# A sparse expert stage between two transformer blocks: the first expert as a unit of its own, gate2 moved to the expert blocks, the late products behind the last down projection

## The chip, the cores and the metric

The kernel runs on 1 core of one Trainium2 chip. The metric is the time of one execution on the device in microseconds, the median of several. The core has a matrix engine (PE, its weight loads shown as PEld), a vector engine (DVE), a scalar engine (ACT), GpSimd (POOL) and a sync engine (SP); 16 DMA engines move data, by queues that SP and POOL fill in this kernel.

## What is computed

512 tokens of width 1024 go through a first block (a mixer, then 32 experts, 4 for each token) and a second block (attention, a gated recurrence, an MLP). The change lies in the experts:

```python
logits = xf @ w_router + b_router
top_val, top_idx = lax.top_k(logits, 4)          # of 32 experts
gates = jax.nn.softmax(top_val, axis=-1)
...
def expert_block(args):                          # 128 rows of one expert e
    xb, e = args
    hu = xb @ w_up[e] + b_up[e]                  # 1024 -> 2048
    x_glu = jnp.minimum(hu[:, :D_FF], 7.0)
    x_lin = jnp.clip(hu[:, D_FF:], -7.0, 7.0)
    act = x_glu * jax.nn.sigmoid(1.702 * x_glu) * (x_lin + 1.0)
    return act @ w_down[e] + b_down[e]           # 1024 -> 1024
ys = lax.map(expert_block, (xs, block_e)).reshape(n_pad, D)
out = segment_sum(ys * row_gate[:, None], row_tok, num_segments=T)
```

The first block then adds `gate2 * out` to the residual, where gate2 is a row of 1024 numbers that the condition gives.

## The kernel before, in words

**Stages.** The mixer runs to about 437 us, the expert stage from there to about 1528, the second block behind it. Everything in the expert stage is in float32. An expert's weights are 8 tiles of `w_up` and 4 of `w_down`, each 128 x 2048 (1 MB); all 32 experts have 384 tiles. `raw` (L296 to L302) fetches one on SP's queue into a ring of 13 buffers, so that a fetch waits until PE has used an older tile.

**Units and steps.** The experts are taken by rank (by how many tokens they have). `UNITS` (L36) lists units of one or two steps: a step is one expert with 128 rows (`_single`), two experts that share a block of 128 rows (`_pair`), or two blocks. Experts 0 and 1 are known by number; from rank 2 on SP reads the expert's number from `Ei` (L1277). For each step `expert_up` makes the up products (L1134, tile `bank_hu`) and the activation; then comes the down projection of the step *before* (`expert_down`, L1134, tile `bank_y`), so that the transposes of one step's activation (`transposed`, L1203, L1204, tile `aT`) are used one step later. At a unit's last step `hot_unit`, `block_rows` and `slots` make the one-hot columns of the next unit, and `gather_unit` gathers its tokens by 64 matmuls with the one-hot columns (L1145, 256 wide: two blocks). `expert_out` multiplies the result by the token's gate (ACT, L1223) into `yb`, and POOL scatters it into `y_d` (L1226), which has four slots for each token. After unit 1 stands a dynamic loop for experts with more rows (L1511; it runs no round here); ahead of it up to 10 tiles of the next unit are fetched.

**The end of the stage.** `expert_bias` loads the residual `xs` (4 tiles of 128 tokens, `h2h` in the rows) and adds the bias part. `add_slots` then loads 8 pairs of pieces of `y_d` by POOL's queue (L1456, tiles `h2l` and `xT`, three pairs of buffers in turn), adds the two (L1457), multiplies by gate2 (`g2bc`, L1458) and adds to `xs` (L1459), two pairs for each `xs`. The last two blocks do not go through `y_d`: `late_rows` transposes their one-hot columns (L1235), and `late_add` makes `yb` = y x gate x gate2 (L1246), splits it in a high and a low part (L1247 on ACT, L1248 on DVE), spreads both over the tokens by products into a `bank_hu` (L1251, L1252) and adds each bank to `xs` (L1253). It is called for the last but one block ahead of the last down projection, and for the last block behind it. Each bank is given back only by its add. The order on PE is that of the code (`pin`); DVE, ACT and POOL run their own queues in the order that the scheduler gives.

Of the kernel before, what the change touches and what calls it, by code (L numbers as in the profile page):

```python
# [7 lines left out]
F = mybir.dt.float32  # L8
# [23 lines left out]
def _pair(a, b, n):  # L32
# [3 lines left out]
UNITS = [  # L36
    [_single(0), _single(1)],
    [_pair(7, 25, 96), _pair(8, 26, 96)],
    [_pair(15, 16, 64), _single(4)],
    [_pair(9, 27, 96), _pair(17, 18, 64)],  # L40
    [[[(2, 0, 128, 0)], [(2, 0, 64, 128), (14, 64, 64, 0)]]],
    [_pair(10, 28, 96), _pair(19, 20, 64)],
    [_pair(11, 29, 96), _single(5)],
    [_pair(12, 30, 96), _pair(21, 22, 64)],
    [[[(3, 0, 128, 0)], [(6, 0, 96, 0), (3, 96, 32, 128)]]],
# [211 lines left out]
def tile_block(ctx, tc, A, out, dbg=None):  # L257
# [846 lines left out]
    hot_unit()  # L1104
    hot0 = [hot_cols(Z[:, :, 64 + b], hot_of(b, (b, 0, 128, 0))) for b in range(2)]
    sel0 = mt([128, 2], "sel0", 1, FR)
# [44 lines left out]

    def gather_unit():
        return gather_T([hots[-1][:, tb] for tb in range(NTB)], 256)

# [43 lines left out]
    def transposed(src):  # L1198
        t = mt([128, 8, 128], "aT", 3, F, mo)
        for k0 in (0, 4):  # L1200
            pt = trbank()
            for k in range(4):
                pin(pe.transpose(pt[:, k * 128:(k + 1) * 128], src[:, (k0 + k) * 128:(k0 + k + 1) * 128], ident))  # L1203
            (vec.tensor_copy if k0 else act.copy)(out=t[:, k0:k0 + 4, :], in_=pt.rearrange("p (k t) -> p k t", k=4))  # L1204
        return t
# [13 lines left out]
    def expert_out(y, sl):  # L1219

        yb = mt([128, 1024], "yb", 2, F, mo)
        for n in range(2):
            act.activation(out=yb[:, n * 512:n * 512 + 512], in_=y[n], func=AF.Copy, scale=sl[1])  # L1223

# [5 lines left out]
    def late_rows(b):  # L1230

        hotT = mt([128, 1024], "ma", 3, FR, mo)[:, 0:512]
        pt = trbank()
        for tb in range(NTB):
            pin(pe.matmul(out=pt[:, tbs[tb]], lhsT=hots[-1][:, tb, 128 * b:128 * b + 128].bitcast(F), rhs=ident,  # L1235
                          start=True, stop=True))
        act.copy(out=hotT, in_=pt)
        return hotT

    def late_add(y, gc, hotT):  # L1240

        yh, yl = (mt([128, 8, 128], "aT", 3, FR, mo).rearrange("p a b -> p (a b)") for _ in range(2))
        t_ = mt([128, 1024], "yb", 2, F, mo)
        for h in range(2):
            hs = slice(h * 512, h * 512 + 512)
            vec.scalar_tensor_tensor(out=t_[:, hs], in0=y[h], scalar=gc, in1=g2bc[:, hs], op0=OP.mult, op1=OP.mult)  # L1246
            act.copy(out=yh[:, hs], in_=t_[:, hs])  # L1247
            vec.tensor_tensor(out=yl[:, hs], in0=t_[:, hs], in1=yh.bitcast(F)[:, hs], op=OP.subtract)  # L1248
            for tb in range(NTB):
                o = pbank("hu")  # L1250
                pin(pe.matmul(out=o, lhsT=hotT[:, tbs[tb]], rhs=yh[:, hs], start=True, stop=False))  # L1251
                pin(pe.matmul(out=o, lhsT=hotT[:, tbs[tb]], rhs=yl[:, hs], start=False, stop=True))  # L1252
                vec.tensor_tensor(out=xs[tb][:, hs], in0=o, in1=xs[tb][:, hs], op=OP.add)  # L1253

# [60 lines left out]
    for src, k in [(ranked(0)[0], k) for k in range(8)] + [(ranked(0)[1], k) for k in range(4)]:  # L1315
        ready[src, k] = raw(src(k))
    X = gather_unit()

# [35 lines left out]
    for n, col in enumerate((RC("p32"), kcol[:, 1:2])):  # L1354
# [14 lines left out]
                             op0=OP.mult, op1=OP.add)  # L1369
    sls = [slots([(0, hot0[b], lambda tb: R[:, tb, b, :])]) for b in range(2)]  # L1370

# [74 lines left out]

    def add_slots():

        spare = mt([128, 8, 256], "xT", 2).rearrange("p a b -> p (a b)")
        pairs_ = [[h2_("l", 0), h2_("l", 1)], [h2_("l", 2), h2_("l", 3)], [spare[:, 0:1024], spare[:, 1024:2048]]]  # L1450
        for tb in range(NTB):
            for j in (0, 2):
                y = pairs_[0]
                pairs_.append(pairs_.pop(0))
                for i, t in enumerate(y):
                    pool.dma_start(out=t, in_=y_d[(j + i) * T + tb * 128:(j + i) * T + tb * 128 + 128, :])  # L1456
                vec.tensor_tensor(out=y[0], in0=y[0], in1=y[1], op=OP.add)  # L1457
                vec.tensor_tensor(out=y[0], in0=y[0], in1=g2bc, op=OP.mult)  # L1458
                vec.tensor_tensor(out=xs[tb], in0=xs[tb], in1=y[0], op=OP.add)  # L1459

    LOOP = 1
    prev = None
    for u, unit in enumerate(UNITS):
        nxt = [blk for step in UNITS[u + 1] for blk in step] if u + 1 < len(UNITS) else []
        sls_, b0 = [], 0
        for n, step in enumerate(unit):
# [9 lines left out]
            if n + 1 == len(unit) and nxt:  # L1476
                X = gather_unit()
            finish = lambda: None
            late = not nxt and n
            if late:  # L1480
                hotT = late_rows(n - 1)
            if prev is not None:
                for y, sl in zip(expert_down(*prev[:2]), prev[2]):
                    finish()
                    if late:
                        late_add(y, sl[1], hotT)
                    else:
                        finish = expert_out(y, sl)
            if u != LOOP or n + 1 < len(unit):
                finish()  # L1490
            prev = (down, [((transposed(a),) + rows[1:], of) for a, (rows, of) in zip(au, blocks)], sls[b0:b0 + len(step)])
            b0 += len(step)
            if not nxt and n == 0:
                expert_bias()
                add_slots()
        sls = sls_
        if u == LOOP:
# [539 lines left out]
```

## Time and profile before

| | |
|---|---|
| median of 3 runs | 2861.84 us (2855.33 to 2865.29) |
| the profiled execution | 2863.78 us, its span 2861.8 |
| busy: PE, DVE, ACT, POOL | 92%, 50%, 27%, 17% |
| chain that ended last: PE, DMA, DVE | 46%, 15%, 12% |
| L1134 products of up / of down | 573.5 / 259.7 us |

A row of the timeline is the start, the time from the first to the last instruction of a run of alike ones, and in brackets how long the engine had idled and what ended that. A row of windows gives the busy time of each engine in a stretch, the clock granted to PE, the share in which the DMA engines were busy, and GB/s.

### The profile page before, as it was taken

The numbers are of one execution on the slowest core, as the hardware profiler recorded it, in microseconds if no ns is written. First come the engines' busy times: TensorE is split into PE (matmuls) and PEld (weight loads), VectorE is DVE, ScalarE is ACT, GpSimd is POOL, SyncE is SP. The second block draws the span as 40 slices with busy tenths as digits, with TensorE's granted clock in tenths as the row PEclk, the third lists the DMA queues.
The fourth block names the chain that finished last, engine by engine and source line by source line (L and its number), as shares of the span: only waits on it lengthen the run. The fifth ranks groups of instructions, "written<-read, shape, count | busy, mean of one in ns | idle before, by whom it ended". The sixth has DMA issues, their size and how long they took to land.

```text
span 2861.8 us, 37210 instructions
## 1 busy us (share of the span) xinstructions
PE 2620.6 (92%) x14592; PEld 1705.2 (60%) x14592; DVE 1419.4 (50%) x2470; ACT 766.5 (27%) x1312; POOL 483.3 (17%) x371
## 2 busy tenths in 40 slices
PE   7999998988999999999948898999988898799997
PEld 4777774433445334334315567777867677688886
DVE  4865573211112111111254668676478888855456
ACT  4432430000000100001004444232235555333231
POOL 1000000000000000000013213333251334422223
PEclk9999998999999999999978998999999899799999
DMA  7355457799999999999983424564323222232231
GB/s 269 111 178 185 149 184 291 306 421 389 421 421 372 422 421 421 421 421 370 421 346 130 157 81 151 175 225 150 98 77 105 72 86 86 70 107 95 89 103 52
DMA packets 128241, 647.34 MB, mean 226 GB/s; under 512 B 16272, under 2 KB 17252, under 8 KB 78912
## 3 DMA queue, kind: packets, MB, share of 16 engines
q1 hardware_dynamic: 121936, 628.07, 57.9%
q0 software_dynamic: 5984, 16.35, 1.5%
q8 instruction: 116, 1.90, 0.3%
q14 instruction: 61, 0.50, 0.1%
q10 hardware_dynamic: 144, 0.52, 0.0%
HBM read 624.42 MB, written 22.12 MB: 226 GB/s over the span
## 4 chain that ended last, share of the span: by engine, by line
PE 46%; DMA 15%; DVE 12%; ACT 2%; issue 2%; POOL 0%; DVEq 0%; SPq 0%; ACTq 0%
PE bank_hu L1134 11%; DMA raw<-in_w_up_dram 6%; PE bank_y L1134 5%; PE bank_d L319 5%; PE bank_d L321 4%; PE bank_d L320 4%; DMA raw<-in_w_down_dram 4%; PE bank_u L321 3%; PE bank_u L319 3%; PE bank_u L320 3%; DVE wl L315 2%; DMA graw<-in_ada_w_dram 2%; PE bank_tr L1145 2%; DMA raw<-in_ada_w_dram 1%; DVE vv L1951 1%
## 5 line engine op out<-in xcount | busy, mean ns | idle before, releaser
L1134 PE MATMUL bank_hu<-raw,xT 128*32 128x512 f32 (+2 forms) x3456 | 573.5, 598 | 13.7 <-DMA raw<-in_w_up_dram 13.7
L1134 PEld LDWEIGHTS bank_hu<-raw,xT 128*32 128x32 f32 (+2 forms) x3456 | 203.2, 124 | 363.1 <-issue 323.6
L315 DVE TENSOR_TENSOR wl<-raw,wh 128x1024 fp32r<-128x1024 f32 (+1 forms) x222 | 315.7, 1431 | 124.7 <-ACT wh L310 123.1
L310 ACT CAST wh<-raw 128x1024 fp32r<-128x1024 f32 (+1 forms) x231 | 236.6, 1042 | 442.6 <-PE bank_u L320 169.9
L1619 POOL TENSOR_TENSOR h2h<-h2h,yt 128x512 f32<-128x512 f32 x161 | 238.2, 1487 | 686.3 <-DVE yt L1618 676.4
L1134 PE MATMUL bank_y<-raw,aT 128*32 128x512 f32 (+2 forms) x1536 | 259.7, 596 | 8.9 <-DMA raw<-in_w_down_dram 8.8
L1191 DVE TENSOR_SCALAR ma<-bank_hu 128x256 f32<-128x256 f32 x80 | 34.0, 425 | 468.2 <-PE bank_hu L1134 468.2
L319 PE MATMUL bank_u<-h_hi,wh 128*128 128x512 f32 (+1 forms) x680 | 253.7, 375 | 5.9 <-ACT h_hi L1603 3.1
L321 PE MATMUL bank_u<-h_hi,wl 128*128 128x512 f32 (+1 forms) x680 | 253.0, 373 | 6.2 <-DVE wl L315 6.2
L320 PE MATMUL bank_u<-h_lo,wh 128*128 128x512 f32 (+1 forms) x680 | 252.6, 372 | 5.8 <-DVE h_lo L1603 5.8
L319 PE MATMUL bank_d<-wh,a 128*128 128x512 f32 x512 | 202.5, 396 | 5.7 <-DVE yt L1618 3.4
L1618 DVE TENSOR_TENSOR yt<-bank_d,G 128x512 f32<-128x512 f32 x168 | 113.2, 686 | 182.9 <-PE bank_d L321 177.2
L320 PE MATMUL bank_d<-wl,a 128*128 128x512 f32 x512 | 200.6, 392 | 0.0
L1192 ACT ACTIVATE mb<-ma 128x256 f32<-128x256 f32 x80 | 33.3, 417 | 619.0 <-DVE ma L1191 612.9
L321 PE MATMUL bank_d<-wh,b 128*128 128x512 f32 x512 | 197.7, 393 | 0.0
L1134 PEld LDWEIGHTS bank_y<-raw,aT 128*32 128x32 f32 (+2 forms) x1536 | 84.3, 124 | 173.2 <-issue 155.4
L1226 POOL DMA_INDIRECT y_d<-yb,ii x18 | 17.7, 984 | 921.0 <-ACT yb L1223 689.7
L321 PEld LDWEIGHTS bank_u<-h_hi,wl 128*128 128x128 f32 x680 | 132.2, 195 | 29.3 <-DVE wl L315 7.0
L320 PEld LDWEIGHTS bank_u<-h_lo,wh 128*128 128x128 f32 x680 | 132.4, 195 | 28.3 <-DVE h_lo L1603 6.4
L319 PEld LDWEIGHTS bank_u<-h_hi,wh 128*128 128x128 f32 x680 | 132.3, 196 | 27.8 <-ACT h_hi L1603 3.3
L1204 DVE COPY aT<-bank_tr 128x512 f32<-128x512 f32 x20 | 13.8, 691 | 246.2 <-PE bank_tr L1203 246.2
L319 PEld LDWEIGHTS bank_d<-wh,a 128*128 128x128 f32 x512 | 96.4, 188 | 31.1 <-DVE yt L1618 5.6
(556 smaller groups left out, 4264.0 us busy)
## 6 DMA issues: line engine op xcount, KB each, us to landing
raw<-in_w_up_dram SPq DMA_DIRECT2D x256, 1024.0 KB, 19.3
raw<-in_w_down_dram SPq DMA_DIRECT2D x128, 1024.0 KB, 19.8
raw<-in_mlp_w_dram SPq DMA_DIRECT2D x128, 512.0 KB, 4.4
graw<-in_ada_w_dram SPq DMA_DIRECT2D x72, 512.0 KB, 4.1
graw<-in_w_ada_dram SPq DMA_DIRECT2D x48, 512.0 KB, 4.7
raw<-in_ada_w_dram SPq DMA_DIRECT2D x24, 512.0 KB, 3.6
raw<-in_rnn_w_in_dram SPq DMA_DIRECT2D x24, 512.0 KB, 4.0
raw<-in_w_in_dram SPq DMA_DIRECT2D x22, 512.0 KB, 4.0
```

Of the source, the lines that this page charges most:

```text
L310: act.copy(out=h, in_=r)
L315: vec.tensor_tensor(out=l, in0=r, in1=h.bitcast(F), op=OP.subtract)
L319: pe.matmul(out=o, lhsT=lhs[0], rhs=rhs[0], start=first, stop=False)
L320: pe.matmul(out=o, lhsT=lhs[0], rhs=rhs[1], start=False, stop=False)
L321: pe.matmul(out=o, lhsT=lhs[1], rhs=rhs[0], start=False, stop=last)
L1134: pin(pe.matmul(out=o[at + a:at + a + tile], lhsT=lhs[:, a:a + tile], rhs=rhs, start=start, stop=stop, tile_position=(0, at + a)))
L1145: pin(pe.matmul(out=pt[:, j * n:j * n + n], rhs=hot[tb], lhsT=h2s[part][tb][:, (k + j) * 128:(k + j + 1) * 128], start=part + tb == 0, sto ...
L1191: vec.tensor_scalar(out=a, in0=hu[:, 0:256], scalar1=7.0, scalar2=None, op0=OP.min)
L1192: act.activation(out=b, in_=a, func=AF.Tanh, scale=0.851)
L1618: vec.tensor_tensor(out=t, in0=ps, in1=G[:, cs], op=OP.mult)
L1619: eng.tensor_tensor(out=xs[tb][:, cs], in0=xs[tb][:, cs], in1=t, op=OP.add)
L1951: vec.tensor_tensor_scan(out=v[:, r], data0=aa[:, o, r], data1=v[:, r], initial=0.0, op0=OP.mult, op1=OP.add)
```

## The change

Four things change.

- Units: expert 0 is a unit alone, and its down projection and `expert_out` come at once; expert 1 goes into the third unit. There are 11 units instead of 10 and so 11 gathers; `gather_unit(n)` gathers 128 columns where the next unit has one block.
- Gate2: `expert_out` now makes `yb` = y x gate x gate2 on DVE, and `add_slots` has no multiply any more.
- `add_slots` is split: pairs 0 to 3 as soon as the residual is there; pairs 4 to 7 on DVE behind the low part of the last but one block.
- The late products of both blocks stand behind the last down projection, each bank sums both blocks, and there are 8 adds to `xs` instead of 16.

```diff
 UNITS = [
-    [_single(0), _single(1)],
+    [_single(0)],
     [_pair(7, 25, 96), _pair(8, 26, 96)],
-    [_pair(15, 16, 64), _single(4)],
-    [_pair(9, 27, 96), _pair(17, 18, 64)],
+    [_single(1), _pair(15, 16, 64)],
+    [_pair(9, 27, 96), _single(4)],
+    [_pair(17, 18, 64), _pair(10, 28, 96)],
     [[[(2, 0, 128, 0)], [(2, 0, 64, 128), (14, 64, 64, 0)]]],
-    [_pair(10, 28, 96), _pair(19, 20, 64)],
-    [_pair(11, 29, 96), _single(5)],
-    [_pair(12, 30, 96), _pair(21, 22, 64)],
+    [_pair(19, 20, 64), _pair(11, 29, 96)],
+    [_single(5), _pair(12, 30, 96)],
+    [_pair(21, 22, 64)],
     [[[(3, 0, 128, 0)], [(6, 0, 96, 0), (3, 96, 32, 128)]]],
     [_pair(23, 24, 64), _pair(13, 31, 96)],
 ]
...
-            act.activation(out=yb[:, n * 512:n * 512 + 512], in_=y[n], func=AF.Copy, scale=sl[1])
+            hs = slice(n * 512, n * 512 + 512)
+            vec.scalar_tensor_tensor(out=yb[:, hs], in0=y[n], scalar=sl[1], in1=g2bc[:, hs], op0=OP.mult, op1=OP.mult)
...
+    def late_products(os, hotT, parts, h, start):
+        for tb in range(NTB):
+            for i in range(2):
+                pin(pe.matmul(out=os[tb], lhsT=hotT[:, tbs[tb]], rhs=parts[i][:, h * 512:h * 512 + 512],
+                              start=start and i == 0, stop=not start and i == 1))
...
+        for j in js:
+            tb, y = j // 2, y_pairs[0]
+            y_pairs.append(y_pairs.pop(0))
+            for i, t in enumerate(y):
+                o = (2 * (j % 2) + i) * T + tb * 128
+                pool.dma_start(out=t, in_=y_d[o:o + 128, :])
+            vec.tensor_tensor(out=y[0], in0=y[0], in1=y[1], op=OP.add)
+            done = vec.tensor_tensor(out=xs[tb], in0=xs[tb], in1=y[0], op=OP.add)
+        return done
...
                     if late:
-                        late_add(y, sl[1], hotT)
+                        with tc.issue_after(added.ins):
+                            parts = [late_parts(y, sl[1], "aT")]
+                        with tc.issue_after(parts[0][2].ins):
+                            add_slots(range(4, 8))
...
+            if u == 0:
+                for y, sl in zip(expert_down(*prev[:2]), prev[2]):
+                    expert_out(y, sl)()
+                prev = None
             if not nxt and n == 0:
                 expert_bias()
-                add_slots()
+                added = add_slots(range(4))
...
-    hotT = late_rows(1)
-    late_add(expert_down(*prev[:2])[0], prev[2][0][1], hotT)
+    y = expert_down(*prev[:2])[0]
+    os = [pbank("hu") for tb in range(NTB)]
+    late_products(os, hotT[0], parts[0], 0, True)
+    parts.append(late_parts(y, prev[2][0][1], "ma"))
+    for h in range(2):
+        if h:
+            os = [pbank("hu") for tb in range(NTB)]
+            late_products(os, hotT[0], parts[0], 1, True)
+        late_products(os, hotT[1], parts[1], h, False)
+        for tb in range(NTB):
+            cs = slice(h * 512, h * 512 + 512)
+            vec.tensor_tensor(out=xs[tb][:, cs], in0=os[tb], in1=xs[tb][:, cs], op=OP.add)
```

SP at the start of the expert stage, before (the first 12 tiles are expert 0's):

```order
L301 DMA raw<-in_w_up_dram 128x2048 x8
L301 DMA raw<-in_w_down_dram 128x2048 x4
L1414 DMA g2bc<-md_d 128x1024
L301 DMA raw<-in_w_up_dram 128x2048
L1277 TENSOR_LOAD Ei
L1277 ISA x2
L1277 TENSOR_LOAD Ei
L1277 ISA x2
```

and after:

```order
L302 DMA raw<-in_w_up_dram 128x2048 x8
L302 DMA raw<-in_w_down_dram 128x2048 x4
L1418 DMA g2bc<-md_d 128x1024
L1281 TENSOR_LOAD Ei
L1281 ISA x2
L1281 TENSOR_LOAD Ei
L1281 ISA x2
L302 ISA
L302 DMA raw<-in_w_up_dram 128x2048
```

The 13th tile, which was expert 1's and stood ahead of the first read of an expert's number, now belongs to a ranked expert and stands behind two such reads.

PE at the end of the stage, before: the last but one down projection (64x512), the first late products, and further on the last down projection (32x512):

```order
L1235 MATMUL bank_tr<-ident,hot 128x128 x4
L1134 MATMUL bank_y<-raw,aT 64x512 x32
L1251 MATMUL bank_hu<-aT,ma 128x512
L1252 MATMUL bank_hu<-aT,ma 128x512
...
L1251 MATMUL bank_hu<-aT,ma 128x512
L1252 MATMUL bank_hu<-aT,ma 128x512
L1203 MATMUL bank_tr<-ident,ma 128x128 x8
L1235 MATMUL bank_tr<-ident,hot 128x128 x4
L1134 MATMUL bank_y<-raw,aT 32x512 x64
```

and after:

```order
L1236 MATMUL bank_tr<-ident,hot 128x128 x8
L1135 MATMUL bank_y<-raw,aT 64x512 x32
L1204 MATMUL bank_tr<-ident,ma 128x128 x8
L1135 MATMUL bank_y<-raw,aT 32x512 x64
L1256 MATMUL bank_hu<-aT,ma 128x512 x8
L1256 MATMUL bank_hu<-ma 128x512 x8
L1256 MATMUL bank_hu<-aT,ma 128x512 x8
L1256 MATMUL bank_hu<-ma 128x512 x8
L1622 MATMUL bank_t<-ident,h2h_9754 128x128 x8
```

The 16 late products between the two down projections now stand behind the last one, with the other 16.

DVE at the same place, before (`yb` and `aT` are the late block's, L1457 to L1459 the pairs):

```order
L1195 SCALAR_TENSOR_TENSOR ma<-bank_hu,ma 128x256
L1246 SCALAR_TENSOR_TENSOR yb<-bank_y,gc,g2bc 128x512 x2
L1248 TENSOR_TENSOR aT<-yb,aT 128x512 x2
L1457 TENSOR_TENSOR h2l_9738<-h2l_9738,h2l_9739 128x1024
L1458 TENSOR_TENSOR h2l_9738<-h2l_9738,g2bc 128x1024
L1459 TENSOR_TENSOR h2h_9680<-h2h_9680,h2l_9738 128x1024
L1457 TENSOR_TENSOR h2l_9740<-h2l_9740,h2l_9741 128x1024
```

and after:

```order
L1196 SCALAR_TENSOR_TENSOR ma<-bank_hu,ma 128x256
L1465 TENSOR_TENSOR h2l_9812<-h2l_9812,h2l_9813 128x1024
L1466 TENSOR_TENSOR h2h_9754<-h2h_9754,h2l_9812 128x1024
L1465 TENSOR_TENSOR h2l_9814<-h2l_9814,h2l_9815 128x1024
L1466 TENSOR_TENSOR h2h_9754<-h2h_9754,h2l_9814 128x1024
L1465 TENSOR_TENSOR xT<-xT 128x1024
L1466 TENSOR_TENSOR h2h_9755<-h2h_9755,xT 128x1024
L1465 TENSOR_TENSOR h2l_9812<-h2l_9812,h2l_9813 128x1024
L1466 TENSOR_TENSOR h2h_9755<-h2h_9755,h2l_9812 128x1024
L1248 SCALAR_TENSOR_TENSOR yb<-bank_y,gc,g2bc 128x512 x2
```

Four pairs of adds now stand ahead of the late block's `yb`, where before all stood behind it.

## Rows read from the trace of the kernel before

**Rows 1.** Windows: stretch, length, busy us by engine, PEclk, DMA share, GB/s

```profile
600.00:1440.00 840.00, 800.97 (x5433) 330.72 (x5425) 156.89 (x390) 68.28 (x132) 21.73 (x24) 0.99 0.99 410
700.00:800.00 100.00, 100.00 (x577) 43.58 (x577) 18.64 (x48) 8.21 (x16) 1.94 (x2) 1.00 1.01 421
1000.00:1100.00 100.00, 89.04 (x654) 33.59 (x650) 17.59 (x45) 6.36 (x13) 1.94 (x2) 1.00 1.01 421
```

**Rows 2.** Chain of waits, 1052 to 1086: start us, us, what

```profile
1059.59 19.86 DMA raw<-in_w_up_dram
...
1079.60 20.38 DMA raw<-in_w_down_dram
```

**Rows 3.** Windows at the front of the stage and at the dynamic loop

```profile
455.00:545.00 90.00, 89.38 (x366) 44.08 (x366) 21.04 (x66) 6.93 (x14) 1.09 (x1) 0.97 0.67 238
640.00:656.00 16.00, 3.37 (x10) 1.26 (x12) 0.94 (x7) 0.00 (x0) 1.03 (x1) 0.53 0.69 270
```

**Rows 4.** Timeline of PE at the end of the stage: start us, us, what, idle before

```profile
1453.67 8.61 PE L1134 MATMUL bank_y<-raw,aT 128*64 128x512 f32 x30 [2.68 <-DMA raw<-in_w_down_dram]
...
1508.54 13.94 PE L1134 MATMUL bank_y<-raw,aT 128*32 128x512 f32 x128
1523.20 0.51 PE L1251 MATMUL bank_hu<-aT,ma 128*128 128x512 f32 x1 [0.72 <-ACT aT L1247]
...
1527.72 1.03 PE L1596 MATMUL bank_t<-ident,h2h 128*128 128x128 f32 x8
```

**Rows 5.** Waits of PE, 1436 to 1532: us in total, times, longest

```profile
PE bank_hu L1251 <- DVE h2h L1253: 35.1, 4, 15.7
```

**Rows 6.** Timeline of POOL: the first reload

```profile
1465.88 0.53 POOL L1456 DMA_DIRECT2D h2l<-y_d  x1 [32.94 <-DVE h2l L1457]
```

**Rows 7.** Instructions of tile raw, 1440 to 1500: the last down tiles

```profile
L301 SPq DMA_DIRECT2D raw<-in_w_down_dram x6: 333/333/333, 1442.5 to 1458.7; - x6
...
DMA to landing us min/median/max: 21.5/23.0/24.1
```

**Rows 8.** Windows at the end of the stage

```profile
1465.00:1475.00 10.00, 0.95 (x4) 0.56 (x3) 9.40 (x9) 0.00 (x0) 2.65 (x5) 0.77 1.02 419
1485.00:1490.00 5.00, 0.00 (x0) 0.00 (x0) 3.73 (x4) 0.00 (x0) 1.06 (x2) 0.50 0.45 149
```

**Rows 9.** Chain of waits, 1436 to 1532: one reload

```profile
1473.06 13.12 DMA h2l<-y_d
```

**Rows 10.** Instructions of tensor y_d, 1420 to 1500: ns min/median/max, and landing

```profile
L1456 POOL DMA_DIRECT2D h2l<-y_d x12: 530/530/591, 1426.9 to 1492.9; - x12
...
DMA to landing us min/median/max: 3.7/9.9/22.8
```

**Rows 11.** Timeline of DVE: one add of a pair

```profile
1464.36 1.22 DVE L1457 TENSOR_TENSOR h2l<-h2l,h2l 128x1024 f32<-128x1024 f32 x1
```

**Rows 12.** Timeline of PE at the front of the stage

```profile
455.54 29.95 PE L1134 MATMUL bank_hu<-raw,xT 128*128 128x512 f32 x64
...
517.21 1.04 PE L1145 MATMUL bank_tr<-hot,h2h 128*128 128x256 f32 x4
...
525.21 13.90 PE L1134 MATMUL bank_y<-raw,aT 128*128 128x512 f32 x32
538.94 1.04 PE L1203 MATMUL bank_tr<-ident,ma 128*128 128x128 f32 x8
```

**Rows 13.** Waits of SP's queue, 437 to 560

```profile
SPq L1277 <- DVE yb L1384: 14.7, 1, 14.7
```

**Rows 14.** Timeline of PE: narrow products with 128x128 weights

```profile
411.70 1.87 PE L1020 MATMUL bank_tr<-wra,h2T 128*128 128x32 f32 x16
```

**Rows 15.** Timeline of DVE: the last block's yb

```profile
1521.69 1.64 DVE L1246 SCALAR_TENSOR_TENSOR yb<-bank_y,gc,g2bc 128x512 f32<-128x512 f32 x2 [13.74 <-PE bank_y L1134]
```

**Rows 16.** Groups by line, 600 to 1440: busy us, mean ns, idle before

```profile
L1223 ACT ACTIVATE yb<-bank_y,gc 128x512 f32<-128x512 f32 x28 | 19.3, 688 | 220.5 <-PE bank_y L1134 220.5
L1204 DVE COPY aT<-bank_tr 128x512 f32<-128x512 f32 x16 | 11.1, 691 | 218.8 <-PE bank_tr L1203 218.8
```

More of the change, by code (lines that the diff above doesn't have):

```diff
@@ L1104, in tile_block @@
     hot_unit()
-    hot0 = [hot_cols(Z[:, :, 64 + b], hot_of(b, (b, 0, 128, 0))) for b in range(2)]
+    hot0 = hot_cols(Z[:, :, 64], hot_of(0, (0, 0, 128, 0)))
     sel0 = mt([128, 2], "sel0", 1, FR)
@@ L1150, in gather_T, with gather_unit @@
         return X
-    def gather_unit():
-        return gather_T([hots[-1][:, tb] for tb in range(NTB)], 256)
+    def gather_unit(n):
+        return gather_T([hots[-1][:, tb, 0:128 * n] for tb in range(NTB)], 128 * n)
     def products(o, rows, k, ws, start, stop):
@@ L1198, in transposed @@
     def transposed(src):
-        t = mt([128, 8, 128], "aT", 3, F, mo)
+        t = mt([128, 1024], "aT", 3, F, mo).rearrange("p (a b) -> p a b", a=8)
         for k0 in (0, 4):
@@ L1230, in late_rows @@
     def late_rows(b):
-        hotT = mt([128, 1024], "ma", 3, FR, mo)[:, 0:512]
         pt = trbank()
@@ L1236, in late_rows, with late_parts @@
                           start=True, stop=True))
+        hotT = hotTs[:, 512 * b:512 * b + 512]
         act.copy(out=hotT, in_=pt)
         return hotT
-    def late_add(y, gc, hotT):
-        yh, yl = (mt([128, 8, 128], "aT", 3, FR, mo).rearrange("p a b -> p (a b)") for _ in range(2))
+    def late_parts(y, gc, tag):
+        yh, yl = (mt([128, 1024], tag, 3, FR, mo) for _ in range(2))
         t_ = mt([128, 1024], "yb", 2, F, mo)
@@ L1247, in late_add @@
             act.copy(out=yh[:, hs], in_=t_[:, hs])
[L1248 to L1253, printed above, removed]
+            done = vec.tensor_tensor(out=yl[:, hs], in0=t_[:, hs], in1=yh.bitcast(F)[:, hs], op=OP.subtract)
+        return yh, yl, done
+    def late_products(os, hotT, parts, h, start):
[3 more added lines that the diff above has]
+                              start=start and i == 0, stop=not start and i == 1))
     def expert_w(ex):
@@ L1316, in tile_block @@
         ready[src, k] = raw(src(k))
-    X = gather_unit()
+    X = gather_unit(1)
     vec.tensor_copy(out=key[:, 1, :], in_=pp[:, 128:160])
@@ L1369, in tile_block @@
                              op0=OP.mult, op1=OP.add)
-    sls = [slots([(0, hot0[b], lambda tb: R[:, tb, b, :])]) for b in range(2)]
+    sls = [slots([(0, hot0, lambda tb: R[:, tb, 0, :])])]
     at = mt([128, 1], "at")
@@ L1445, in expert_bias, with add_slots @@
             vec.tensor_tensor(out=xs[tb], in0=xs[tb], in1=bt, op=OP.add)
[L1447 to L1459, printed above, removed]
+    y_pairs = []
+    def add_slots(js):
+        if not y_pairs:
+            spare = mt([128, 8, 256], "xT", 2).rearrange("p a b -> p (a b)")
+            y_pairs.extend([[h2_("l", 0), h2_("l", 1)], [h2_("l", 2), h2_("l", 3)],
+                            [spare[:, 0:1024], spare[:, 1024:2048]]])
+        for j in js:
[7 more added lines that the diff above has]
+        return done
     LOOP = 1
@@ L1476, in tile_block @@
             if n + 1 == len(unit) and nxt:
-                X = gather_unit()
+                X = gather_unit(len(nxt))
             finish = lambda: None
@@ L1480, in tile_block @@
             if late:
-                hotT = late_rows(n - 1)
+                hotTs = mt([128, 1024], "ma", 3, FR, mo)
+                hotT = [late_rows(b) for b in range(2)]
             if prev is not None:
```

## The prediction

> **What bounds the kernel now.** I read the table of windows over the expert stage first. From 600 to 1440 us the DMA engines are busy for 0.99 of the time at 410 GB/s, and in 700 to 800 and in 1000 to 1100 for all of it at 421 GB/s [rows 1]. PE is nearly as full, 801 of 840 us, but it is PE that waits: in 1000 to 1100 it is busy for 89.04 of 100. The chain of waits shows the same from the other side: link after link is one weight tile's transfer, each released by the one eight tiles before it, 19.86 and 20.38 us a link [rows 2], so 2.5 us for a tile of 1 MB. So the middle of the stage runs at the pace of the 384 weight tiles, and PE time saved there buys nothing. Something is to be had only where the DMA engines idle, or where PE goes on after the last tile is there.
>
> There are two such places. At the front (455 to 545 us) the DMA share is 0.67 [rows 3], so 90 x (1.01 - 0.67) / 1.01 = 30 us of transfer time are lost: the ring of 13 buffers is full and PE frees it at its own pace. At the tail I read PE's timeline [rows 4]. The last but one down projection ends at 1462.3, the last one starts only at 1508.54 and then runs its 128 products in 13.94 us without a wait. Between them PE waits four times for DVE, 35.1 us in all [rows 5]: a late product needs a bank, the bank needs the add L1253, and this add stands on DVE's queue behind pairs of add_slots whose reloads were issued only after the first pairs had been added. The first reload went out at 1465.88, after 32.94 us of waiting for DVE [rows 6], since the first add stood behind the late block's yb.
>
> **The change, part by part.**
>
> *Late products behind the last down projection.* The four waits and the products between the two down projections leave this place. What is late next is the last weight tile. The last tile of w_down was issued at 1458.7, and such tiles landed 21.5 to 24.1 us later, median 23.0 [rows 7], so it was there at 1481.7, long before PE asked for it. The DMA share says the same: 1.02 in 1465 to 1475 and 0.45 in 1485 to 1490 [rows 8]. After the change PE takes these tiles as they land; behind the last one come the products of one or two tiles, 13.94 / 8 = 1.7 us each, so 1.7 to 3.5; I take 2.6. If nothing else moved, the last down projection would end at 1484.3 and not at 1508.54 + 13.94 = 1522.5: 38.2 us.
>
> *Reloads that now go ahead of the last tiles.* Add_slots reloads 8 pairs of 0.5 MB pieces of y_d through three pairs of buffers; pairs 3 to 7 each wait for an earlier pair's adds. Before, the ten reloads began at 1465.88; the one issued at 1473.06 landed 13.12 us later, at 1486.2 [rows 9], behind the last tile, and so did the five after it. After, DVE has the adds of pairs 0 to 3 ahead of the late block's yb, so pairs 3 to 6 are asked for some 15 to 20 us earlier and pair 7 right after the late parts. Six more loads, 3.1 MB, then share the engines while the last tiles are under way: 3.1 MB / 421 GB/s = 7.5 us if all of it comes first, 0 if none does. Reloads landed after 9.9 us in the median and weight tiles after 23 [rows 7, 10], so reloads do get through first: I take 7.5. By the Trainium skill (DMA: Bandwidth & Descriptors, section "Queues, rings and completion order") each DMA engine takes turns, packet by packet, between the queues that have work, so that a reload beside one weight queue gets half of the engines; by that rule the term is the whole 7.5 too, but a reload would land in about 2.5 us (an estimate by that page, half of 421 GB/s), and the median of 9.9 does not show it.
>
> *Do the adds still hold up the last block?* DVE's queue has the adds of pairs 4 to 7 ahead of the last block's yb. Pair 7 is asked for when pair 4 has been added, about 6 us after the end of the last but one down projection. That end moves with the front and with the early reloads to about 1465, so the loads go out at about 1471, land at 1481 by the median of 9.9 and at 1484 by 13.12, and their two adds (1.22 us each [rows 11]; the multiply by gate2 is gone) end at 1483 to 1487. The last down projection ends at 1488, so they are just covered, by 1 to 5 us; this is the thin place.
>
> *The end.* Before, the last block's late products, half as many, brought PE to bank_t 1527.72 - 1522.5 = 5.2 us after the last down projection [rows 4]. Now 16 of the 32 products more stand there: 8 fill the wait for yb, the other 8 cost 8 x (1527.72 - 1523.20) / 16 = 2.3 us, and the banks of the second half must be freed by the adds of the first. I take 7.6, so 2.4 us are lost here (0 to 4).
>
> *Front.* Expert 0 alone: its up (29.95 us for 8 tiles [rows 12]) frees tiles more slowly than 8 x 2.55 = 20.4 us of transfer, as before: 9.5 us idle. Then come lists, the gather for the next unit (517.21 to 525.21, 8.0 us), the transposes (1.04) and the wait for their copies, about 13.5 us in which no tile is freed, and the down projection (13.90 for 4 tiles, 3.7 idle). That is 27. By the same count before was 9.5 + 3.6 (lists) + 8 (up of expert 1) + 8 (gather) + 3.7 = 33, measured 30. So 6 are recovered. Against it: the 13th tile was expert 1's, known by number, and issued right behind the first 12; now it is ranked, and stands behind SP's wait of 14.7 us for DVE's list [rows 13], so its 2.5 us of transfer come later, in idle time that is counted. Left are about 4 us, bounds 0 and 7. The extra gather (11 in place of 10) takes 64 matmuls bound by their weight loads: 128-wide ones are no cheaper than 1.87 / 16 = 0.117 us each [rows 14], so 7.5 us, as much as a wide one. This is PE time, and so are about 2 us of waiting before the first down projection; both lie in the 39 us that PE had free between 600 and 1440 [rows 1], some 17 of them at the dynamic loop. At the dynamic loop 8 tiles instead of 10 are on their way while PE stands; the share was 0.69 there [rows 3], so I count 0, and at most 2 x 2.55 = 5 lost.
>
> *Gate2 at the blocks.* Two DVE operations of 0.82 us [rows 15] replace two ACT ones of 0.688, and the DVE half of aT, 0.69, stands behind them [rows 16]. PE's next work is a whole up projection (29.95 us for expert 0's [rows 12]) and DVE is busy for 157 of 840 us [rows 1], so I count 0; without that cover it would be 18 x 2.3 = 41. On DVE 8 multiplies of 1.2 us go; they stood on the chain that is gone already.
>
> **The sum**, against the profiled execution's own 2863.8 us: 1481.7 - 4 (front) + 7.5 (reloads) + 2.6 = 1487.8 for the end of the last down projection instead of 1522.5, so 34.7 us less; less 2.4 for the end: 32.3, which gives 2831.5. The profiled execution lay 1.9 above the median of the runs shown, so 2829.6; I forecast 2829.
>
> **The rivals.** *A: the reload chain holds the last block.* If pair 7's load takes the longest landing seen, 22.8 us [rows 10], it ends at 1494, the adds at 1496.5, and yb starts 9 us later than forecast: 2838. For it: the cover is thin, and all reloads now meet the weight tiles. Against: the median. [...]
> *B: the front gives nothing.* The late 13th tile and the loop's shorter prefetch use up what expert 0 recovers, or PE's 10 added us become the bound in a stretch where it is full: 4 + 5 us worse, 2838. For it: PE is busy for all of 700 to 800 [rows 1].
> *C: better.* The early reloads fit into time that the engines have anyway, and the weights do not come later: 7.5 better, 2822, and down to 2816 with the upper bound of the front and nothing lost at the end. For it: the share is below 1 in places of the stage.
> *D: slower.* Gate2 on DVE comes on PE's path at every block: 18 x 2.3 = 41, with the gather's 7.5 and the 2 us of the first down projection 51 lost, 32.3 won: 2863.8 + 18.7 - 1.9 = 2881. It decides once PE needs aT within 2.3 us of a down projection's end; against it stands the up projection in between.
>
> **How the numbers follow.** Forecast (2823 to 2836) 0.50; C 0.17; A 0.13; B 0.14; D 0.03; nothing moves, because the tail turns out to wait on another thing, 0.03. The range from 2816 to 2842 takes in the bounds of the front, the reloads and the end, and most of A, B and C. A measurement of this kernel can tell about 0.3%, 8.6 us, from no change: faster than 2853.2 is 0.94, within it 0.03, slower 0.03.
>
> **What would show it.** Right: no wait of PE for an add on the residual between the last two down projections; the last one runs in pieces with waits for raw and ends near 1488; the front's DMA share rises; aT is never waited for but at expert 0. Wrong on A: PE's late products wait for yb while DVE waits for y_d. Wrong on B: the share from 600 to 700 falls, or PE has no waits for weights left before 1400. Wrong altogether, if the last down projection still starts after 1500.

## The result and the profile after

The changed kernel took 2836.78 us (median of 4 runs, 2827.93 to 2840.16); the kernel before, in the same measurement, 2862.66 (4 runs, 2855.33 to 2865.29). The ratio is 0.9897, 95% interval 0.9875 to 0.9918: faster, by 26 us. The forecast was 2829, with a range of 2816 to 2842. The profiled execution of the changed kernel took 2827.93, the shortest of its four; its span is 2826.0.

The middle of the stage still runs at the pace of the weight tiles. Windows of the changed kernel, for 600 to 1440 and 1000 to 1100 (as rows 1), the front (as rows 3) and the last tiles (as rows 8); the columns are those of rows 1:

```profile
600.00:1440.00 840.00, 817.88 (x5306) 340.31 (x5308) 187.75 (x434) 49.36 (x104) 22.61 (x25) 0.99 0.99 407
1000.00:1100.00 100.00, 100.00 (x662) 41.03 (x660) 19.91 (x47) 5.09 (x11) 1.94 (x2) 1.00 1.01 421
455.00:545.00 90.00, 86.76 (x518) 40.51 (x518) 24.31 (x82) 5.58 (x12) 1.09 (x1) 0.96 0.71 271
1465.00:1475.00 10.00, 5.74 (x38) 1.20 (x38) 3.04 (x4) 1.04 (x2) 0.53 (x1) 1.00 1.02 419
1485.00:1490.00 5.00, 3.05 (x24) 0.69 (x16) 2.19 (x2) 0.00 (x0) 0.00 (x0) 0.88 0.96 363
```

PE is busy for longer than before (817.88 of 840 us against 800.97, [rows 1]) and the DMA engines are now busy up to 1490, where before they were half idle from 1485 on [rows 8]. The timeline of PE at the end of the stage, as rows 4:

```profile
1463.72 1.10 PE L1204 MATMUL bank_tr<-ident,ma 128*128 128x128 f32 x8
1466.09 1.06 PE L1135 MATMUL bank_y<-raw,aT 128*32 128x512 f32 x6 [1.28 <-ACT aT L1205]
1467.66 4.80 PE L1135 MATMUL bank_y<-raw,aT 128*32 128x512 f32 x32 [0.51 <-DMA raw<-in_w_down_dram]
...
1475.18 5.34 PE L1135 MATMUL bank_y<-raw,aT 128*32 128x512 f32 x32 [2.71 <-DMA raw<-in_w_down_dram]
1482.71 5.34 PE L1135 MATMUL bank_y<-raw,aT 128*32 128x512 f32 x32 [2.19 <-DMA raw<-in_w_down_dram]
1490.03 3.62 PE L1135 MATMUL bank_y<-raw,aT 128*32 128x512 f32 x26 [1.98 <-DMA raw<-in_w_down_dram]
1493.58 2.11 PE L1256 MATMUL bank_hu<-aT,ma 128*128 128x512 f32 x8
...
1501.14 1.04 PE L1622 MATMUL bank_t<-ident,h2h 128*128 128x128 f32 x8
```

The two last down projections follow each other; the last one starts at 1466 instead of 1508.54 and runs in pieces, all but the first released by weight tiles. PE's waits from 1400 to 1520 say the same: the 35.1 us for the adds [rows 5] are gone, and what is late next is the weights.

```profile
PE bank_y L1135 <- DMA raw<-in_w_down_dram: 14.7, 7, 2.7
```

The pieces come every 7.5 us, and so do the pairs of reloads. DVE's timeline of the same stretch:

```profile
1446.04 1.23 DVE L1465 TENSOR_TENSOR h2l<-h2l,h2l 128x1024 f32<-128x1024 f32 x1 [5.01 <-DMA h2l<-y_d]
...
1453.51 1.23 DVE L1465 TENSOR_TENSOR xT<-xT 128x1024 f32<-128x1024 f32 x1 [4.98 <-DMA xT<-y_d]
...
1461.10 1.23 DVE L1465 TENSOR_TENSOR h2l<-h2l,h2l 128x1024 f32<-128x1024 f32 x1 [5.11 <-DMA h2l<-y_d]
...
1490.05 1.23 DVE L1465 TENSOR_TENSOR h2l<-h2l,h2l 128x1024 f32<-128x1024 f32 x1 [2.87 <-DMA h2l<-y_d]
1491.31 1.22 DVE L1466 TENSOR_TENSOR h2h<-h2h,h2l 128x1024 f32<-128x1024 f32 x1
1492.83 1.61 DVE L1248 SCALAR_TENSOR_TENSOR yb<-bank_y,gc,g2bc 128x512 f32<-128x512 f32 x2 [0.29 <-PE bank_y L1135]
```

A pair of reloads (1.05 MB) and two weight tiles (2.1 MB) are 3.15 MB, and 3.15 MB / 421 GB/s = 7.5 us: the step in which both DVE and PE advance. The last pair was added at 1492.5, and the last block's yb followed at 1492.83, released by PE: the reloads were just covered.

Start times differ from run to run (the first weight tile was asked for between 414.6 and 418.3 us), so the experiments are compared from that issue on. The table gives, from the profile of each, the issue of the expert stage's first weight tile, the start of PE's last piece that waited for a weight (the last tile has landed; in brackets, the landing itself where PE came later), the end of the last down projection, the first bank_t, and the latter counted from the first issue:

| kernel | first issue | last tile | last down ends | bank_t | after the issue |
|---|---|---|---|---|---|
| before | 415.67 | (1482.8) | 1522.5 | 1527.72 | 1112.1 |
| changed | 414.62 | 1490.03 | 1493.7 | 1501.14 | 1086.5 |
| changed, again (e5) | 414.88 | 1491.37 | 1498.0 | 1505.44 | 1090.6 |
| units alone (e1) | 415.46 | (1479.2) | 1517.9 | 1523.13 | 1107.7 |
| all but the units (e2) | 417.57 | 1493.53 | 1497.2 | 1504.62 | 1087.1 |
| gate2 alone (e3) | 415.76 | (1483.4) | 1516.2 | 1521.43 | 1105.7 |
| no reloads (e4) | 416.16 | 1479.64 | 1483.3 | 1490.74 | 1074.6 |
| adds behind (e6) | 415.17 | 1479.83 | 1483.5 | 1519.72 | 1104.6 |
| two pairs last (e7) | 418.33 | 1489.19 | 1492.8 | 1500.30 | 1082.0 |
| two pairs last, POOL (e8) | 416.44 | 1485.03 | 1488.7 | 1498.27 | 1081.8 |
| gate2 back (e9) | 415.41 | 1489.14 | 1492.8 | 1510.81 | 1095.4 |

The landings in brackets come from the last tile's own row; in the kernel before it is the issue at 1458.7, and the tile took the longest of the six in [rows 7]:

```profile
L301 SPq DMA_DIRECT2D raw<-in_w_down_dram x1: 333/333/333, 1458.7 to 1458.7; - x1
...
DMA to landing us min/median/max: 24.1/24.1/24.1
```

So it landed at 1482.8, and not at the 1481.7 of the prediction.

### The profile page after: what moved, and what is told of

The parts are those of the page before. It is cut to its first block, busy times and chain, and to the rows that moved or that the text cites. A ratio compares the mean times of both kernels' runs of the same rounds, so it can differ in the third digit from the quotient of the medians.

```text
span 2826.0 us, 37313 instructions
## 1 busy us (share of the span) xinstructions
PE 2633.7 (93%) x14656; PEld 1711.5 (61%) x14656; DVE 1433.9 (51%) x2492; ACT 744.0 (26%) x1278; POOL 484.8 (17%) x371
## 4 chain that ended last, share of the span: by engine, by line
PE 54%; DMA 10%; DVE 10%; ACT 2%; issue 2%; POOL 0%; DVEq 0%; SPq 0%; ACTq 0%
PE bank_hu L1135 14%; PE bank_y L1135 6%; PE bank_d L320 5%; PE bank_d L322 5%; PE bank_d L321 5%; DMA raw<-in_w_up_dram 4%; PE bank_u L322 4%; PE bank_u L320 4%; PE bank_u L321 4%; DMA raw<-in_w_down_dram 3%; PE bank_tr L1146 2%; DVE wl L316 2%; DVE vv L1977 1%; DVE h2h L1659 1%; DMA graw<-in_ada_w_dram 1%
## 5 line engine op out<-in xcount | busy, mean ns | idle before, releaser
L1135 PEld LDWEIGHTS bank_hu<-raw,xT 128*32 128x32 f32 (+2 forms) x3456 | 197.4, 124 | 361.8 <-issue 340.8
L1645 POOL TENSOR_TENSOR h2h<-h2h,yt 128x512 f32<-128x512 f32 x161 | 238.7, 1490 | 675.8 <-DVE yt L1644 665.9
L1225 DVE SCALAR_TENSOR_TENSOR yb<-bank_y,gc,g2bc 128x512 f32<-128x512 f32 x32 | 24.0, 751 | 207.7 <-PE bank_y L1135 205.7
```

What stands on the lines that cost most here:

```text
L1135: pin(pe.matmul(out=o[at + a:at + a + tile], lhsT=lhs[:, a:a + tile], rhs=rhs, start=start, stop=stop, tile_position=(0, at + a)))
L1645: eng.tensor_tensor(out=xs[tb][:, cs], in0=xs[tb][:, cs], in1=t, op=OP.add)
```

## The experiments

**The new units alone, and all but the units.** In e1 the units of the changed kernel, the gather of 128 columns and this clause stand in the kernel before:

```diff
+            if u == 0:
+                for y, sl in zip(expert_down(*prev[:2]), prev[2]):
+                    expert_out(y, sl)()
+                prev = None
```

> The new units alone, on the kernel before: expert 0 a unit by itself with its down projection at once, expert 1 in the third unit, 11 gathers; gate2, add_slots and the late products as before. If the front gives back the 4 us of the prediction, the last weight tile lands 4 us earlier, but the tail of before waits for DVE's adds anyway, and the time changes by 0 to -4 us. If the late 13th tile and the shorter prefetch at the dynamic loop use it up (rival B, and what the profile of the changed kernel looks like), the idle transfer time from 437 to 700 us is the same as before or 0 to 5 us more, and the total is 0 to 5 us longer.

e2 is the reverse: the changed kernel with the old units.

```diff
-    [_single(0)],
+    [_single(0), _single(1)],
...
-            if u == 0:
-                for y, sl in zip(expert_down(*prev[:2]), prev[2]):
-                    expert_out(y, sl)()
-                prev = None
```

> The other half: gate2 at the blocks, add_slots split, late products behind the last down projection, but the units of before. If the whole gain is the tail's, this is as fast as the changed kernel or up to 3 us faster (ratio to before 0.988 to 0.991), and the last down projection ends some 29 us earlier than in the kernel before. If the front gave 4 us of the gain, this one is 4 us slower than the changed kernel.

e1 took 2861.09 us against 2868.37 of before, ratio 0.9978 (0.9963 to 0.9994); e2 2841.45, ratio 0.9900 (0.9872 to 0.9928). So the tail with gate2 brings nearly all of it, and the units alone a little: 7 us by the medians, where 0 to 4 were expected. In e2 the last down projection ended 25 us earlier than before, not 29. In e1 PE's waits for the adds are as before, and the whole tail is only a few us earlier:

```profile
PE bank_hu L1252 <- DVE h2h L1254: 33.8, 4, 13.2
```

Counted from the first issue bank_t came 4.4 us earlier in e1 than before, and the last weight tile landed 3.4 us earlier (1063.7 against 1067.1), close to the 4 us of the prediction. But with the new tail the units are worth little: the last tile landed 1075.4 us after the first issue in the changed kernel and 1076.0 in e2. Where the gain went is seen in the two-block step (2, 14). Windows of 900 to 1000 and 940 to 950, of e1 first, then of the changed kernel:

```profile
900.00:1000.00 100.00, 98.39 (x597) 39.67 (x594) 18.00 (x49) 8.79 (x17) 1.93 (x2) 1.00 0.93 381
940.00:950.00 10.00, 9.67 (x88) 4.26 (x89) 1.10 (x8) 0.00 (x0) 0.00 (x0) 1.00 1.00 415
```

```profile
900.00:1000.00 100.00, 98.42 (x584) 40.06 (x582) 21.04 (x53) 6.26 (x13) 1.94 (x2) 0.97 0.91 368
940.00:950.00 10.00, 9.89 (x73) 4.65 (x75) 0.85 (x7) 0.00 (x0) 0.00 (x0) 0.66 0.99 411
```

The granted clock is 0.66 in 940 to 950, right after PE had waited 1.0 and 0.3 us for DVE. The step's next gather then starts at 972.53 instead of 969.70, the full ring holds up the DMA engines that much longer, and (381 - 368) / 421 x 100 = 3.1 us of transfer are lost again. That accounts for most of the 4 us. A third profile bears it out: in e8 (below), with the new units, gate2 at the blocks and a clock of 1.00 in 940 to 950, this gather starts 554.9 us after the first issue, as in e1 (554.2), against 557.9 in the changed kernel.

**Gate2 alone.**

```diff
-            act.activation(out=yb[:, n * 512:n * 512 + 512], in_=y[n], func=AF.Copy, scale=sl[1])
+            vec.scalar_tensor_tensor(out=yb[:, hs], in0=y[n], scalar=sl[1], in1=g2bc[:, hs], op0=OP.mult, op1=OP.mult)
...
-                vec.tensor_tensor(out=y[0], in0=y[0], in1=g2bc, op=OP.mult)
```

> Gate2 alone: the gate row is multiplied in at the blocks on DVE, the multiply in add_slots goes, all else as before. Forecast: nothing at the blocks; at the tail DVE's chain of adds, on which PE waits, loses 8 multiplies of 1.2 us, so the second of the two last down projections starts up to 9 us earlier: 0 to -9 us. Rival D (DVE's two operations and the copy of aT come on PE's path at every block): up to 41 us slower.

2857.33 us, ratio 0.9959 (0.9941 to 0.9976). The total is 11 us shorter by the medians, a little more than the 0 to 9 expected; bank_t came 6.4 us earlier after the first issue. At the blocks it cost nothing that shows (the last tile landed 1067.6 us after the first issue, before 1067.1), and at the tail PE waited 28.0 us for the adds instead of 35.1.

```profile
PE bank_hu L1252 <- DVE h2h L1254: 28.0, 4, 15.3
```

Rival D, gate2 on PE's path at every block, is out.

**The reloads left out.** The residual then lacks five of eight pairs.

```diff
-                        with tc.issue_after(parts[0][2].ins):
-                            add_slots(range(4, 8))
...
-                added = add_slots(range(4))
+                added = add_slots(range(3))
```

> The changed kernel with pairs 3 to 7 of the slots left out: their ten loads of 0.5 MB and their ten adds are not made, so the residual lacks these parts. If the reloads take their bytes from the weight tiles, the last tile lands 5.2 MB / 421 GB/s = 12.5 us earlier than in the changed kernel and the last two down projections wait less between their pieces. If the reloads only fill time that is free anyway, the last tile lands at the same time, within 2 us.

One run, 2834.97 us, too few for a verdict on the total; the trace decides. PE's last piece that waited for a weight:

```profile
1479.64 3.62 PE L1135 MATMUL bank_y<-raw,aT 128*32 128x512 f32 x26 [1.30 <-DMA raw<-in_w_down_dram]
```

That is 1063.5 us after the first issue, against 1075.4 in the changed kernel: 11.9 us for ten loads whose bytes are 12.5 us. The reloads take their time from the weight tiles, nearly byte for byte; there is no free time for them there, and rival C is out.

**The changed kernel again.**

> The changed kernel once more, beside new runs of before and with a profile of its own. The second block, which the change does not touch, took 1334.1 us in the profile of before (from bank_t to the end) and 1324.9 in that of the changed kernel. If this is chance (the granted clock of a run), it now lies anywhere from 1325 to 1343, and the ratio stays at 0.987 to 0.992 while bank_t starts 26 to 27 us earlier than before again. If the change itself shortens the second block, it stays near 1325.

2835.38 us against 2871.14, ratio 0.9875 (0.9858 to 0.9891): the same as the first measurement within the intervals. The second block took 1328.3 us here (2833.7 - 1505.44), 1324.9 in the first profile, 1334.1 before, and from 1328.8 to 1342.5 in e1 to e4. So some of the 9 us by which it was shorter in the first profile are not the new tail's: with the old tail it took 1328.8 in e1. Both branches of the expectation hold 1328.3, and the changed kernel's two profiles have the two shortest second blocks of all eleven, so whether the change has a part in them stays open. The other half of the expectation failed: bank_t came 22.3 us earlier than before (21.5 counted from the first issue), not 26 to 27, while the medians differ by 36. In this run the last piece of the last down projection took 6.59 us instead of 3.62, at a granted clock of 0.54 (1490 to 1497); timeline and windows:

```profile
1491.37 6.59 PE L1135 MATMUL bank_y<-raw,aT 128*32 128x512 f32 x26 [2.59 <-DMA raw<-in_w_down_dram]
```

```profile
1485.00:1490.00 5.00, 3.63 (x28) 0.63 (x16) 3.36 (x3) 0.00 (x0) 0.00 (x0) 1.00 1.00 391
1490.00:1497.00 7.00, 5.63 (x25) 1.31 (x26) 2.71 (x3) 0.00 (x0) 0.00 (x0) 0.54 0.71 275
```

PE had worked in pieces between waits for 45 us when the clock fell (so it had in the first profile, where this piece took 3.62), and this piece has nothing behind it that hides 3 us.

**All adds behind the late block.**

```diff
-                        with tc.issue_after(added.ins):
-                            parts = [late_parts(y, sl[1], "aT")]
-                        with tc.issue_after(parts[0][2].ins):
-                            add_slots(range(4, 8))
+                        parts = [late_parts(y, sl[1], "aT")]
+                        with tc.issue_after(parts[0][2].ins):
+                            add_slots(range(8))
...
-                added = add_slots(range(4))
```

> The changed kernel, but all eight pairs of adds stand behind the late block's low part on DVE, as they did before, so that nine of the ten reloads cannot go out until the last weight tiles have nearly landed. If reloads and weight tiles share the engines byte for byte, the last down projection ends 7 to 10 us earlier than in the changed kernel (at 1484 to 1487 instead of 1493.65), but the reloads then end the stage: 5 MB or 12.5 us behind the last tile, with their adds, so that the total is 3 to 10 us longer than the changed kernel's. If reloads cost the weights nothing, the last down projection ends where it did and the total is 10 us or more longer.

2851.20 us, ratio 0.9932 (0.9908 to 0.9956), 16 us longer than the changed kernel and not 3 to 10. The weights land 10.7 us earlier after the first issue than in the changed kernel, and the old wait is back, at the late products, 24.5 us in all:

```profile
1479.83 3.62 PE L1135 MATMUL bank_y<-raw,aT 128*32 128x512 f32 x26 [1.27 <-DMA raw<-in_w_down_dram]
...
1491.69 1.22 PE L1256 MATMUL bank_hu<-aT,ma 128*128 128x512 f32 x2 [3.99 <-DVE h2h L1544]
1500.42 1.22 PE L1256 MATMUL bank_hu<-aT,ma 128*128 128x512 f32 x2 [7.51 <-DVE h2h L1544]
1508.03 1.22 PE L1256 MATMUL bank_hu<-aT,ma 128*128 128x512 f32 x2 [6.39 <-DVE h2h L1544]
1515.88 1.22 PE L1256 MATMUL bank_hu<-aT,ma 128*128 128x512 f32 x2 [6.63 <-DVE h2h L1544]
```

bank_t starts 18 us later than in the changed kernel (14 later than in e5). But DVE did not run the order that was meant. It stood for 15.78 us and took the first add only behind the first half of the last block's yb, at 1483.29, where the kernel before has it at 1464.36 [rows 11] and the changed kernel at 1438.54:

```profile
1482.62 0.75 DVE L1248 SCALAR_TENSOR_TENSOR yb<-bank_y,gc,g2bc 128x512 f32<-128x512 f32 x1 [15.78 <-PE bank_y L1135]
1483.29 1.21 DVE L1465 TENSOR_TENSOR h2l<-h2l,h2l 128x1024 f32<-128x1024 f32 x1
```

So all ten reloads go out from 1484.80 on, behind the last tile: e6 has the price of the reloads for the weights once more, and it shows that with late adds the wait moves to the late products. What moving the products alone brings, with the first add where it was before, no run shows.

**Two pairs behind the weights.** Two attempts at a better version. In e7 pairs 6 and 7 are loaded by SP's queue behind the last weights and added after the late products' adds; in e8 their four adds go to POOL.

```diff
-                            add_slots(range(4, 8))
+                            add_slots(range(4, 6))
...
+    with tc.issue_after(done.ins):
+        add_slots(range(6, 8), sync)
```

> The changed kernel, but pairs 6 and 7 (four loads of 0.5 MB) are asked for by SP behind the last weight tiles, and their adds stand behind the eight adds of the late products on DVE. If ten early reloads cost the weights 10.4 us, four fewer give back 4.2: the last down projection ends near 1489.5 and bank_t starts near 1497. The four adds (4.9 us on DVE) then delay only the last quarter of the residual: total 0 to 4 us shorter than the changed kernel. If DVE becomes the bound of the tail, 0 to 3 us longer.

> As the kernel with pairs 6 and 7 loaded by SP behind the last weight tiles, but their four adds on POOL instead of DVE. There the last down projection ended 4.5 us earlier after the first weight's issue than in the changed kernel, and DVE's four late adds gave it back (second group of bank_t at the same time). If that was the reason, DVE is now free, the second group of bank_t starts 3 to 5 us earlier than in the changed kernel and the total is 2 to 5 us shorter than its 2835 to 2837. If POOL, which also splits weights there, delays the last quarter of the residual, the total is the same or up to 5 us longer.

e7 took 2841.02 us (ratio 0.9893, 0.9876 to 0.9909; the changed kernel beside it 0.9875), e8 2844.95 (0.9923, 0.9901 to 0.9945); both are longer than either expectation allowed. The forecast of the first half held: the last down projection ended 4.5 us earlier after the first issue in e7 and 6.8 in e8, where the two-block step had kept its clock and the last tile was asked for 1.8 us earlier. The rest did not come through. The second group of bank_t waits for ACT; changed kernel, e7, e8:

```profile
1507.17 1.12 PE L1622 MATMUL bank_t<-ident,h2h 128*128 128x128 f32 x4 [4.99 <-ACT hf L1626]
```

```profile
1510.43 1.11 PE L1624 MATMUL bank_t<-ident,h2h 128*128 128x128 f32 x4 [9.09 <-ACT hf L1628]
```

```profile
1517.65 1.11 PE L1625 MATMUL bank_t<-ident,h2h 128*128 128x128 f32 x4 [18.22 <-ACT hf L1629]
```

In both ACT's queue has been given another order than in the changed kernel. In e7 the activation that PE waits for stands behind two more casts of attention weights, the first of which waited 2.54 us for its load, and the late adds on DVE stand ahead of the split of these weights; in e8 it stands behind one that waits for a load (ada_w, 7.05 us). So e8 does not test whether DVE was the reason in e7: that stays open. Neither beats the changed kernel.

**Gate2 put back.**

```diff
-            vec.scalar_tensor_tensor(out=yb[:, hs], in0=y[n], scalar=sl[1], in1=g2bc[:, hs], op0=OP.mult, op1=OP.mult)
+            act.activation(out=yb[:, n * 512:n * 512 + 512], in_=y[n], func=AF.Copy, scale=sl[1])
...
             vec.tensor_tensor(out=y[0], in0=y[0], in1=y[1], op=OP.add)
+            vec.tensor_tensor(out=y[0], in0=y[0], in1=g2bc, op=OP.mult)
```

> The changed kernel with gate2 put back: expert_out multiplies by the token's gate alone, on ACT, and add_slots multiplies each of the 8 pairs by gate2 on DVE (1.22 us each). Since DVE now waits 2 to 6 us for each reloaded pair, the multiplies should be hidden for pairs 0 to 6, and only pair 7's stands ahead of the last block's yb: 0 to 2.5 us longer than the changed kernel. If gate2 at the blocks carries the gain, the total is 6 us or more longer, as much as gate2 alone gave on the kernel before. The granted clock in the two-block step (900 to 1000 us) was 0.97 in all profiles that had both the new units and gate2 at the blocks, 1.00 in the others: if gate2 on DVE is part of the cause, it is 1.00 here and the last weight tile lands about 3 us earlier.

2846.09 us against 2865.53, ratio 0.9924 (0.9905 to 0.9944): some 10 us longer than the changed kernel, the 6 or more of the expectation and not the 0 to 2.5. (The profiled execution took 2856.64, the longest of its four; the others took 2845.01 to 2846.46.) Here rival A happens. The last reload goes out at 1490.94 instead of 1478.86, and PE waits for the last block's yb; POOL, PE and DVE:

```profile
1490.94 0.53 POOL L1463 DMA_DIRECT2D h2l<-y_d  x1 [15.17 <-DVE h2h L1466]
```

```profile
1502.62 4.08 PE L1255 MATMUL bank_hu<-ma 128*128 128x512 f32 x8 [7.82 <-ACT ma L1248]
```

```profile
1484.88 1.23 DVE L1464 TENSOR_TENSOR h2l<-h2l,h2l 128x1024 f32<-128x1024 f32 x1 [2.44 <-DMA h2l<-y_d]
1486.02 1.22 DVE L1465 TENSOR_TENSOR h2l<-h2l,g2bc 128x1024 f32<-128x1024 f32 x1
...
1489.42 2.35 DVE L1466 TENSOR_TENSOR h2h<-h2h,h2l 128x1024 f32<-128x1024 f32 x2
```

The last tile landed 1.7 us earlier after the first issue than in the changed kernel, but bank_t came 8.9 us later (4.8 later than in e5). The multiplies cost more than their own time: in the order that the scheduler gave DVE here, the add that frees the buffer for the last reload stands behind three multiplies and behind the adds of two later pairs, the second of which waits for its load until 1484.88. In the changed kernel it stood behind one such add, and ran at 1477.35. So gate2 at the blocks is not a side gain of 0 us, as the sum had it: with this order it keeps the reload chain ahead of the last block. The granted clock in 940 to 950 is 0.66 here as well, so gate2 is not what lowers it.

## Why the prediction was right, and where it was off

The forecast was a gain of 32.3 us up to bank_t; the profiles show 1112.1 - 1086.5 = 25.5 counted from the first issue. The direction, the place and the mechanism are the forecast's: the four waits for the adds end, the last weight tile is late next, and it is the reloads, moved ahead, that make it later. By terms:

- *Front*, 4 forecast. Right for the units alone (3.4 at the last tile and 4.4 at bank_t in e1), but 0.5 beside the new tail (the last tile against e2's), since the lower clock in the two-block step lost 3.1 us of transfer again. The working overlooked two things that the trace after shows. The first gather, now 128 wide, took longer than the wide one: it ran from 436.48 to 450.16, 13.7 us, at 1.05 us a group of four throughout, where the wide one took 9.8.

```profile
436.48 1.08 PE L1146 MATMUL bank_tr<-hot,h2h 128*128 128x128 f32 x4 [2.27 <-DVE key L1325]
...
449.31 1.05 PE L1146 MATMUL bank_tr<-hot,h2l 128*128 128x128 f32 x4
```

  And the list that SP waits for comes from the engines behind it, so that the wait [rows 13] became longer, and the 13th tile was asked for at 457.20:

```profile
SPq L1281 <- DVE yb L1388: 19.8, 1, 19.8
```

- *The last tile of before*, 1481.7 in the sum, from the median landing. It landed at 1482.8, 1.1 later: 1067.1 after the first issue and not 1066.0.
- *Reloads*, 7.5 forecast. From 1067.1 to 1075.4 are 8.3, and with the front's 0.5 the reloads cost 8.8. The price for a byte was right (11.9 measured in e4 for 12.5 of bytes), and so, nearly, was the count: four of the ten reloads were taken to have been ahead of the last tile in the kernel before already; there three had landed by 1482.8 and the fourth landed at 1484.4.
- *Last tiles*, 2.6 forecast (1.7 to 3.5): the last piece took 3.62, the two tiles of the upper bound; 6.59 in e5.
- *End*, 7.6 forecast from the last down projection to bank_t: 1501.14 - 1493.65 = 7.5.
- *Gate2 at the blocks*, 0 forecast: 0 at the blocks, as e3 shows, but at the tail it was worth more than nothing (e9).

The sum with what was measured: 1067.1 - 0.5 + 8.8 + 3.6 + 7.5 = 1086.5, the table's number. Against the forecast's terms the front lost 3.5, the last tile of before 1.1, the reloads 1.3 and the last tiles 1.0, together 6.9; the end gave back 0.1. So the front is the term that was mis-sized most, and the clock in the two-block step was no part of the forecast. That the totals agree better than this is in part luck: the profile at 2827.93 is even below the sum's 2831.5, since its first issue came 1.1 us earlier and its second block, of which the forecast said nothing, was 9.2 us shorter than in the profile of before. In e5 the medians differ by 36 us, more than forecast, while bank_t gained 21.5.

Of the rivals, A did not happen here but was as close as said (the last pair's add ended 0.3 us before yb), and in e9 PE waits 7.8 us for yb; B's loop cost nothing new, since the share in the changed kernel's loop, 0.86 over 30 us, is as much idle time as before (0.69 over 16 us), and from 545 to 700 us the DMA engines moved 405 GB/s against 404 before:

```profile
590.00:620.00 30.00, 17.99 (x95) 7.15 (x88) 3.06 (x9) 0.58 (x1) 0.99 (x1) 0.77 0.86 343
```

On the reloads' landing the trace went away from both numbers of the prediction: not 9.9 us and not 2.5 but 17.3 in the median, from 1410 to 1500; below it, what SP's queue of weights (q1) and POOL's queue of reloads (q0) moved from 1440 to 1485, in packets, MB and share of the engines' time:

```profile
DMA to landing us min/median/max: 8.1/17.3/23.5
```

```profile
q1 hardware_dynamic: 1717, 12.50, 66.9%
q0 software_dynamic: 1721, 6.26, 34.8%
```

The Trainium skill (DMA: Bandwidth & Descriptors, section "Queues, rings and completion order") has each DMA engine take turns between its queues, packet by packet. The trace agrees: by the profile's count the two queues moved 1717 and 1721 packets. But a row of a weight tile is 8 KB and a row of a reload 4 KB, and the bytes went 12.50 to 6.26 MB, two to one; the prediction's half of the engines took the packets to be alike. At a third of 421 GB/s a reload's 0.5 MB take 3.7 us, and the rest of the 17.3 us is its wait behind other reloads of its own queue: they landed one every 3.8 us. The Trainium skill (SBUF — State Buffer, section "SBUF: two separate sides") has POOL kept from writing its DMAs' descriptors by DVE copies of certain modes, but not by additions of two tensors as here. The trace agrees: a reload's issue took 527 to 591 ns, also beside an add of DVE (the issue at 1440.06).

## What to carry to other kernels

When a stretch is bound by bytes, moving a load out of a wait moves its bytes in front of something else: count every load that the change lets go earlier at its full price, less those that had landed ahead already, and read the last landing itself where the trace has it. Two queues that both have work need not share by halves: here the bytes went by the size of their packets. A chain of load, add and reload through few buffers is set by the adds' places on their engine: with the first add at 1483.29 (e6) instead of 1438.54, bank_t came 14 to 18 us later. And work that looks free on an engine with slack (here the multiplies) may change the order in which such a chain runs, and cost more than its own time.

## What the runs showed that was not expected

The granted clock fell to 0.66 in 940 to 950 in the changed kernel, e4, e5, e6 and e9, to 0.73 in e7, and stayed at 1.00 there in e1 and e8 (both with the new units) and in the three with the old units. Just before it PE had waited 1.0 and 0.3 us for DVE in e1 as well, so this wait alone does not decide it; what does, stays open. It cost the changed kernel 3 to 4 us.

A gather of 64 products 128 columns wide took 13.7 us at the start of the stage where one of 256 columns took 9.8: in the narrow one the group time stayed at 1.05 us, in the wide one it fell to 0.64 half way. In the stretch 437 to 447 the granted clock was 0.50, the lower level, in the changed kernel and 0.70 before.
